# RWKV core and attention of a hybrid encoder: block-diagonal operands replaced by compact 64x64 ones, and the two pairs of heads worked in turn

## The chip, the cores and the metric

One core of one Trainium2 chip. The metric is the device time of one execution in microseconds (us), as the median of several runs; lower is better. The engines are TensorE (PE; its weight loads are PEld), VectorE (DVE), ScalarE (ACT), GpSimd (POOL) and SyncE (SP), which issues most of the transfers.

## The reference, cut to what matters

Two layers over 256 tokens of width 1024. Each layer has a token mixer and a channel mixer (a dense SwiGLU in the first layer, top-2-of-8 experts in the second), each behind a norm and a modulation from a condition vector (the "ada" weights). The token mixer projects its input (`w_in`) to four groups of 256 columns: 2-D neighbourhood attention with 4 heads of 64, bidirectional RWKV-7 with 4 heads of 64, a multi-scale pooling and a gated short convolution; the four outputs go through one output projection (`w_out`). The change touches the first two groups. RWKV is, for each head and each of the two directions:

```python
def rwkv7_step(S, inp):
    r, w, k, v, a_vec, b_vec = inp
    sa = jnp.einsum('...ij,...j->...i', S, a_vec)
    S = S * w[..., None, :] + sa[..., :, None] * b_vec[..., None, :] + v[..., :, None] * k[..., None, :]
    return S, jnp.einsum('...ij,...j->...i', S, r)
```

Attention takes for each query the keys of its row neighbourhood and 16 columns, adds a bias, and does a softmax. In the kernel that is a score matrix of 128 queries by 256 keys with a bias of -1e30 outside the window.

## The kernel before, in words

All activations are float32. Large weights come in chunks of 128 x 2048 (1 MB) through SP's queue into a ring `raw`, and are split into a high part (ScalarE, L220) and a rest (VectorE, L221); a product with them is three one-pass matmuls (`mm3`, L172). The "ada" chunks are multiplied and reduced on VectorE (L257). `mm` (L169) is a full float32 matmul.

`mixer(l)` (L361) is written as generators, one for each part of the work: `z` (RWKV projections), `q` and `r` (`rw_prep`, L470, for head pair 0 and 1), `0` and `1` (`rw_core`, L536, for pair 0 and 1), `a` (attention, L705), `p` (pooling), `c` (convolution), `f` (ada chunks as filler), `g`, and `o` (the output projection, L670). Each `yield` ends a step. A string `ORDER[l]` (L62) says which part does its next step, a letter a step; `step` (L885) first finishes the parts that one depends on (`needs`, L881). The string sets the priority; a scheduler at compile time then orders each engine's instructions by it and by when it holds their inputs to be ready. In `ORDER` of before, pair 0's core stands early, among the projections of attention, and pair 1's core late, among the output projection; each core has 41 steps.

A pair of heads is stacked on the 128 partitions: head 0 on 0 to 63, head 1 on 64 to 127. `rw_core` works on four chunks of 64 tokens (c) in two directions (e). To do both heads in one 128x128 matmul, `rw_prep` writes block-diagonal 128x128 copies of four operands (`bd4`, L374; `put_bd`, L385), with zeros from GpSimd and two ScalarE copies each. In `rw_core`:

- `s1`, `s3`, `s2` (L547 on, L580 on): products of the operands. `s1` and `s2` have 128 moving columns (two 64-column operands of `ar`).
- five levels that build the inverse of a triangular matrix (L560 on): VectorE transposes X (L563), `p1` = nT x X (L566), ScalarE copies it to P1 (L568), `p2` = XT x P1 (L573), VectorE writes it under a mask into X (L574). In the trace `p1` and `p2` are both named p.
- between the levels, transposes of three operands through TensorE (`sk`, L593).
- the recurrence over four chunks (L600 on), all in `u`: a product, a copy (L610), a product, a copy (L612), two products, and the new state (L623, L625).
- the outputs `y` (L629 on): per head a 64-column weight against 64 columns.

`slot_` (L365) gives buffers of 128 x 512 from a ring of 47. PSUM has two sets of four banks, `pa` and `pb`; pair 0's core and the RWKV projections use `pb`, attention, convolution and pooling `pa`. `bk` (L533) says which set a core takes; with `SWITCH` (0, 0) pair 1's core takes `pa` for its first step alone. The output projection holds the four banks of `pa` from its first step to the end. Attention (L705) pads the queries of each head with zeros (`qz`, L713), computes two heads' scores into one bank (L741), and multiplies with values for both heads of the pair (L759), of which half is used.

The mixers stand at the start of the two layers; the dense FFN follows the first, the experts (MoE) follow the second.

Of the kernel before, what the change touches and what calls it, by code (L numbers as in the profile page):

```python
# [48 lines left out]
_CST = [("ident", 128), ("i2", 64), ("bones", 128), ("bones64", 128), ("m1s", 256), ("m1i", 128), ("m3", 256),  # L49
# [4 lines left out]
for _n, _w in _CST:  # L54
# [22 lines left out]
def _constants():  # L77
# [10 lines left out]
    t2 = np.concatenate([t, t])  # L88
    same = h[:, None] == h[None]
    c["m1s"] = np.concatenate([same & (s[:, None] < t2), same & (s[:, None] > t2)], axis=1) * 1.0  # L90
    c["m1i"] = np.concatenate([s[:, None] <= t, s[:, None] >= t], axis=1) * 1.0
    c["m3"] = np.concatenate([same & (t2 < s[:, None]), same & (t2 > s[:, None])], axis=1) * 1.0
# [18 lines left out]
    lx = np.zeros((128, NLV + 1, 2, 128))  # L111
    for l in range(-1, NLV):
        b = 1 << (l + 1)
        sb, tb = s[:, None] // b, t2[None] // b
        up = (sb % 2 == 0) & (tb == sb + 1)
        dn = (sb % 2 == 1) & (tb == sb - 1)
        lx[:, l + 1, 0] = up & same
        lx[:, l + 1, 1] = dn & same
# [5 lines left out]
def kernel(ctx, tc, x, cc, cst, cst2, msk, ada, pcol, lora, poolw, rpb, win, winl, wout,  # L124
# [15 lines left out]
    mk = per.tile([128, (NLV + 1) * 256], U8, name="mk")  # L140
# [220 lines left out]
    def mixer(l, fillers):  # L361
        with ExitStack() as st:
# [11 lines left out]
            def bd4(name):  # L374
                b = slot_(name).rearrange("p (n h t) -> p n h t", n=4, h=2)
                pool.memset(b[0:64, :, 1, :], 0.0)
                pool.memset(b[64:128, :, 0, :], 0.0)
                return b

            def flat(b, n):  # L380
                return b[:, n].rearrange("p h t -> p (h t)")
# [3 lines left out]
            def put_bd(b, src):  # L385
                for h in range(2):
                    act.activation(b[HS[h], :, h, :], src[HS[h]], AF.Copy)
# [82 lines left out]
            def rw_prep(hp):  # L470
# [45 lines left out]
                B = {n: [] for n in "ABKV"}  # L516
# [10 lines left out]
            m1s = C("m1s").rearrange("p (e h t) -> p e h t", e=2, h=2)  # L527
            m1i = C("m1i").rearrange("p (e t) -> p e t", e=2)
            m3 = C("m3").rearrange("p (e f) -> p e f", e=2)
# [6 lines left out]
            def rw_core(hp):  # L536
                R = st_r[hp]
                ar, B, bc = R["ar"], R["B"], R["bc"]
                arb = n8("arb")
                ark = n8("ark")  # L540
                X, nT, XT, ak, sB, sK, sV, Ub, Sb = [[None, None] for _ in range(9)]
                for e in range(2):
                    X[e] = v4(slot_("X"))
                    act.activation(X[e], ident[:, None, :].to_broadcast([128, 4, 128]), AF.Copy)
                    p = bk[hp]("s1").rearrange("p (c m t) -> p c m t", c=4, m=2)
                    for c in range(4):
                        mm(p[:, c], flat(B["B"][e], c), ar[e][:, c])  # L547
# [5 lines left out]
                    for c in range(4):  # L553
                        mm(p[:, c], flat(B["A"][e], c), flat(B["B"][e], c))
# [4 lines left out]
                for lv in range(NLV):  # L559
                    pt = [None, None]  # L560
# [945 lines left out]
```

## Time and profile before

| | us |
|---|---|
| median of 3 runs | 1547.24 |
| lowest and highest | 1546.98, 1551.23 |
| the profiled execution | 1546.37 |
| its span, first to last instruction | 1544.5 |
| PE busy | 1443.1 |
| DVE busy | 645.8 |
| ACT busy | 435.5 |
| POOL busy | 24.9 |

All rows come from one profiled execution of 1546.37 us. Busy time is the union of the instructions of an engine. Matmuls are pipelined: an instruction's length reaches over the start of the next ones, so how fast a stream runs is read from the distance of their starts. A float32 matmul shows as two instructions. In a row of instructions, `128*64 128x64` after the names means 128 rows by 64 columns of weights against 64 moving columns. Tile names come without their numbers.

### The profile page before, as it was taken

Reading aid. Unit: us, or ns where it says so; the run is one execution under the profiler, and the core shown is the slowest. Engines: PE = TensorE matmul, PEld = TensorE weight load, DVE = VectorE, ACT = ScalarE, POOL = GpSimd, SP = SyncE. Lnnn points to the kernel's source line nnn. Section 1 sums busy time; section 2 is a strip of 40 time slices with the busy share of each in tenths; the row PEclk is TensorE's granted clock in tenths of the full one; section 3 lists DMA queues with packets and bytes.
Section 4 is the critical chain, followed back from the end, with each engine's and each line's share of the span. In section 5 each row is a group of like instructions: output and inputs, shape, how many; then the busy total and the mean of one; then the engine's idle time right before and its main releaser. Section 6 shows DMA issues by size and latency. Waiting matters only on the chain. (4 is left out here: it accounts for less than half of the span.)

```text
span 1544.5 us, 28342 instructions
## 1 busy us (share of the span) xinstructions
PE 1443.1 (93%) x12174; PEld 875.5 (57%) x12174; DVE 645.8 (42%) x1194; ACT 435.5 (28%) x814; POOL 24.9 (2%) x91
## 2 busy tenths in 40 slices
PE   3999989999998999989889899999999999998885
PEld 2988979999997999963223233433433234332222
DVE  7799869977856777651010021020020110110202
ACT  4854645544437746350011000010010010000101
POOL 1001000000001001000000000000000000000000
PEclk9999999999999999999999999999999999999998
DMA  9556138987743411189999999999999999999995
GB/s 373 215 204 227 55 146 340 394 339 306 293 158 122 158 55 42 45 323 363 416 415 416 417 417 417 416 415 382 412 417 416 417 415 416 416 415 416 416 410 194
DMA packets 85253, 487.79 MB, mean 316 GB/s; under 512 B 9841, under 2 KB 10225, under 8 KB 40946
## 3 DMA queue, kind: packets, MB, share of 16 engines
q1 hardware_dynamic: 83522, 482.98, 78.3%
q10 hardware_dynamic: 1584, 2.68, 0.6%
q8 instruction: 113, 1.85, 0.5%
q14 instruction: 34, 0.28, 0.0%
HBM read 484.57 MB, written 1.05 MB: 314 GB/s over the span
## 5 line engine op out<-in xcount | busy, mean ns | idle before, releaser
L170 PE MATMUL u<-mw,xe 128*32 128x512 f32 (+1 forms) x3368 | 359.0, 537 | 20.1 <-DMA mw<-in_moe_dram 18.7
L1179 DVE TENSOR_TENSOR sg<-sg,u 128x256 f32<-128x256 f32 (+1 forms) x96 | 34.3, 380 | 650.6 <-ACT sg L1178 650.6
L170 PEld LDWEIGHTS u<-mw,xe 128*32 128x32 f32 x3368 | 114.5, 109 | 220.8 <-issue 160.4
L1178 ACT ACTIVATE sg<-u 128x256 f32<-128x256 f32 (+1 forms) x96 | 30.8, 355 | 666.0 <-PE u L170 656.5
L170 PE MATMUL y<-mw,sT 128*32 128x512 f32 x1480 | 180.4, 594 | 15.5 <-DMA mw<-in_moe_dram 10.8
L221 DVE TENSOR_TENSOR wlo<-raw,whi 128x1024 fp32r<-128x1024 f32 x142 | 169.8, 1218 | 46.7 <-ACT whi L220 46.5
L220 ACT ACTIVATE whi<-raw 128x1024 fp32r<-128x1024 f32 x142 | 146.4, 1056 | 137.1 <-issue 43.6
L170 PE MATMUL u<-mwhi,xe 128*32 128x512 f32 (+1 forms) x748 | 172.6, 551 | 0.4 <-PEq L1132 0.3
L170 PE MATMUL u<-mwlo,xe 128*32 128x512 f32 (+1 forms) x748 | 150.7, 551 | 0.5 <-PEq L1132 0.2
L174 PE MATMUL g<-hlo,whi 128*128 128x256 f32 x448 | 126.9, 284 | 0.5 <-DVE hlo L339 0.3
L173 PE MATMUL g<-hhi,whi 128*128 128x256 f32 x448 | 126.9, 284 | 0.0
L175 PE MATMUL g<-hhi,wlo 128*128 128x256 f32 x448 | 126.6, 283 | 0.0
L170 PEld LDWEIGHTS y<-mw,sT 128*32 128x32 f32 x1480 | 52.5, 109 | 128.0 <-issue 84.7
L257 DVE CUSTOM_DVE_ANT_0 raw<-raw,row,pcs 128x1024 f32<-128x1024 f32 x96 | 120.3, 1278 | 4.5 <-ACT row L1362 3.9
L170 PE MATMUL y<-mwhi,sT 128*32 128x512 f32 x324 | 96.2, 594 | 0.1
L173 PE MATMUL z<-hhi,whi 128*128 128x256 f32 x304 | 88.9, 293 | 4.1 <-ACT whi L220 4.0
L170 PEld LDWEIGHTS u<-mwhi,xe 128*32 128x32 f32 x748 | 46.2, 109 | 79.7 <-issue 70.0
L175 PE MATMUL z<-hhi,wlo 128*128 128x256 f32 x304 | 88.1, 290 | 2.2 <-DVE wlo L221 2.2
L174 PE MATMUL z<-hlo,whi 128*128 128x256 f32 x304 | 87.6, 289 | 0.5 <-DVE hlo L339 0.3
L174 PEld LDWEIGHTS g<-hlo,whi 128*128 128x128 f32 x448 | 85.9, 192 | 1.6 <-DVE hlo L339 1.2
L173 PEld LDWEIGHTS g<-hhi,whi 128*128 128x128 f32 x448 | 86.0, 192 | 0.6
L175 PEld LDWEIGHTS g<-hhi,wlo 128*128 128x128 f32 x448 | 85.9, 192 | 0.0
(317 smaller groups left out, 2022.8 us busy)
## 6 DMA issues: line engine op xcount, KB each, us to landing
mw<-in_moe_dram SPq DMA_DIRECT2D x232, 1024.0 KB, 15.0
mwlo<-in_moe_dram SPq DMA_DIRECT2D x104, 512.0 KB, 12.6
mwhi<-in_moe_dram SPq DMA_DIRECT2D x104, 512.0 KB, 13.8
raw<-in_ada_dram SPq DMA_DIRECT2D x44, 1024.0 KB, 6.7
raw<-in_ffn_dram SPq DMA_DIRECT2D x42, 1024.0 KB, 7.1
raw<-in_win_dram SPq DMA_DIRECT2D x20, 1024.0 KB, 4.9
raw<-in_wout_dram SPq DMA_DIRECT2D x6, 1024.0 KB, 5.0
raw<-in_ada_dram SPq DMA_DIRECT2D x8, 512.0 KB, 7.1
```

Of the source, the lines that this page charges most:

```text
L170: pe.matmul(o, a, b, start=start, stop=stop)
L173: pe.matmul(o, ah, bh, start=start, stop=False)
L174: pe.matmul(o, ah, bl, start=False, stop=False)
L175: pe.matmul(o, al, bh, start=False, stop=stop)
L220: ops[0].append(act.activation(hi, raw[:, c], AF.Copy))
L221: ops[1].append(dve.tensor_sub(lo, raw[:, c], hi.bitcast(F32)))
L257: r = dve.tensor_tensor_reduce(w, w, cB, scale=1.0, scalar=P(l, "ab", v * KB + k), op0=OP.mult, op1=OP.add, accum_out=mods[l][:, v, k:k + 1])
L1178: other_set(act.activation(sg, u[:, 0:w], AF.Silu))
L1179: dve.tensor_mul(sg, sg, u[:, w:2 * w])
```

## The change

Every product of the RWKV core becomes two 64x64 products, for the two heads, on the two diagonal quarters of the array; the operands stay compact, 64 columns wide in place of 128, in a second ring of 38 buffers of 128 x 256 (`half`). `bd4` and `put_bd` go. The transposes `sk` become products with a 64x64 identity. Masks and constants are 64 columns wide. Attention's queries are copied in one piece; the two heads' scores are 64-row products into two banks, with two bias additions; the value product takes a head's 64 columns. `ORDER` is new: the projections first, then steps of both cores in turn. The last piece but one of the output projection is a part of its own, `O`, that waits for core 0; `o` no longer waits for it. `SWITCH` (99, 99) keeps pair 1's core on `pa` until `o` starts. The ring of 128 x 512 buffers has 36. The reserve of SBUF for descriptors is cut to 1024 bytes.

```diff
-NSLOT = 47
+NSLOT = 36
+NHALF = 38
-ORDER = (('00zzzzqqqaqaq0a00a0a0a00000pp00a000a00000pa00f000a00af00000a0000rcarf00rfrffccrcfffffo11gf'
-          '11101111111111111111111111111111111o1o1111foffoooooooofffffffffffffffff'),
-         ('zzzqqaqqfa0aqa0000pa000a0000000a00p000ap0000az00000a0a0000001crar0ra00110crr1c0go1c1111111'
-          '1111111111111111111111o11o11o11o1ooooooo'))
-SWITCH = (0, 0)
+ORDER = (('zzzzqaqaqaqrcrcrcrp00010a101a01f010f10p101a01a010f10c101a01f010f101a01p010a10f101f01a010a10f101f01a01fg'
+          '010f101o01o010f101o01o010f101o01o'),
+         ('zzzzqaqaqaqrcrcrcrp0001010a1010a1010p10101a0101a0101c01010a1010a1010p10101a0101a0101a0101a010o101o01'
+          '0o101o010o101o010o101o'))
+SWITCH = (99, 99)
...
+            def half(name):
+                return mp.tile([128, 256], F32, name=name, tag="h", bufs=NHALF).rearrange("p (n f) -> p n f", n=4)
+            def mmh(o, a, b, start=True, stop=True):
+
+                for h in HS:
+                    mm(o[h], a[h], b[h], start, stop)
...
-                for e in range(2):
-                    for n, src in (("B", c4(bc)[:, e]), ("A", ar[e][:, :, 0, :]), ("K", c4(kf)[:, e]),
-                                   ("V", c4(zv)[:, e])):
-                        b = bd4("bd" + n)
-                        put_bd(b, src)
-                        B[n].append(b)
-                    yield
-                st_r[hp] = dict(eP=eP, ar=ar, bc=c4(bc), B=B)
+                st_r[hp] = dict(eP=eP, ar=ar, B=c4(bc), K=c4(kf), V=c4(zv))
+                yield
...
-                        pt[e] = v4(bk[hp]("p1"))
+                        p = pq("p1")
                         for c in range(4):
-                            mm(pt[e][:, c], nT[e][:, c], X[e][:, c])
-                        P1[e] = v4(slot_("P1"))
-                        act.activation(P1[e], pt[e], AF.Copy)
+                            mmh(p[:, c], nT[e][:, c], X[e][:, c])
+                        P1[e] = half("P1")
+                        act.activation(P1[e], p, AF.Copy)
...
-                                pe.transpose(p[:, c], flat(B[nm][e], c), ident)
-                            b = v4(slot_("s" + nm))
+                                mmh(p[:, c], R[nm][:, e, c], C("i2"))
+                            b = half("s" + nm)
...
-                        mm(pu[:, 0], ak[e][:, c], sV[e][:, c], True, i == 0)
+                        mmh(pu[:, 0], ak[e][:, c], sV[e][:, c], True, i == 0)
...
-                    for h in range(2):
-                        for j, (a, b) in enumerate(seq):
-                            mm(yp[HS[h], c * 64:(c + 1) * 64], a[:, HS[h]], b, j == 0, j == len(seq) - 1)
+                    for j, (a, b) in enumerate(seq):
+                        mmh(yp[:, c * 64:(c + 1) * 64], a, b, j == 0, j == len(seq) - 1)
...
-                        p = pa("sc").rearrange("p (h t) -> p h t", h=2)
+                        s = et("sc")
+                        ps = [pa("sc") for _ in range(2)]
                         for h in range(2):
-                            mm(p[:, h, :], qz[hp][:, h, qs], kt[:, hp, :])
-                        s = et("sc")
-                        dve.tensor_add(s, p, bi)
+                            mm(ps[h][:, 0:T], qt[HS[h], hp, qs], kt[HS[h], hp, :])
+                        for h in range(2):
+                            dve.tensor_add(s[:, h, :], ps[h][:, 0:T], bi[:, h, :])
...
-                                mm(po[:, i, :], pt[:, h, k, :], vn[:, k, hp * 128:(hp + 1) * 128], k == 0, k == 1)
+                                mm(po[:, i, HS[h]], pt[:, h, k, :], vn[:, k, hp * 128 + 64 * h:hp * 128 + 64 * h + 64],
+                                   k == 0, k == 1)
...
-                yield from out_proj(3, yrw, False, False, 0)
...
-                     "f": fill(99), "g": gate_row(), "r": rw_prep(1), "1": rw_core(1), "o": outs()}
-            needs = {"q": "z", "0": "q", "1": "r", "r": "z", "o": "apc0", "g": "f" if l == 0 else ""}
+                     "f": fill(99), "g": gate_row(), "r": rw_prep(1), "1": rw_core(1), "o": outs(),
+                     "O": out_proj(3, yrw, False, False, 0)}
+            needs = {"q": "z", "0": "q", "1": "r", "r": "z", "o": "apc", "O": "0", "g": "f" if l == 0 else ""}
...
-    nc = _bacc.Bacc("TRN2", target_bir_lowering=False, num_devices=1)
+    nc = _bacc.Bacc("TRN2", target_bir_lowering=False, num_devices=1, dynamic_dma_scratch_size=1024)
```

## Rows read from the trace of the kernel before

**Rows 1.** Busy time by stage: a stretch in us from the span's start and its length; then for PE, PEld, DVE, ACT and POOL the busy us and the number of instructions; the granted clock, the DMA share, GB/s. The first mixer, the second, the MoE layer from 700 us on.
```profile
30.00:228.00 198.00, 186.83 (x1500) 174.30 (x1500) 161.69 (x301) 113.91 (x216) 5.03 (x18) 1.00 0.49 176
485.00:671.00 186.00, 182.44 (x1494) 171.46 (x1493) 132.87 (x241) 109.30 (x210) 5.86 (x19) 1.00 0.28 96
700.00:1544.50 844.50, 792.52 (x7247) 276.58 (x7238) 113.77 (x265) 64.18 (x163) 0.00 (x0) 1.00 0.99 404
```
**Rows 2.** What TensorE waited for in the second mixer (485 to 671 us): the waiting engine and tile, the releaser; us in total, times, longest.
```profile
PE lw L170 <- issue: 1.0, 1, 1.0
```
**Rows 3.** The timeline of PE: start, us, engine, line, operation, tiles, shape, count of the instructions merged in the row.
```profile
155.11 0.28 PE L173 MATMUL z<-hhi,whi 128*128 128x256 f32 x1
155.23 0.28 PE L174 MATMUL z<-hlo,whi 128*128 128x256 f32 x1
...
189.09 1.04 PE L593 MATMUL sk<-cs,bdK 128*128 128x128 f32 x8
189.97 1.95 PE L170 MATMUL p<-X,nT 128*128 128x128 f32 x16
191.75 1.45 PE L170 MATMUL p<-P,XT 128*128 128x128 f32 x11
...
571.83 1.03 PE L170 MATMUL sc<-kt,qz 128*128 128x256 f32 x4
572.69 1.05 PE L170 MATMUL u<-sV,ak 128*128 128x128 f32 x8
```
**Rows 4.** The timeline of PE in the output product of pair 1 in the first mixer, where it goes from head 0 to head 1 of a chunk; and one row of the view of the tile y in the first mixer, with the least, median and greatest length in ns, the first and the last start.
```profile
207.93 0.28 PE L170 MATMUL y<-ark,sV 128*64 128x64 f32 x2
...
208.16 0.22 PE L170 MATMUL y<-ark,sV 128*64 128x64 f32 x1
208.16 0.22 PE L170 MATMUL y<-ar,Sb 128*64 128x64 f32 x1
208.22 0.22 PE L170 MATMUL y<-arb,Ub 128*64 128x64 f32 x1
208.22 0.22 PE L170 MATMUL y<-ar,Sb 128*64 128x64 f32 x1
...
L170 PE MATMUL y<-arb,Ub x64: 222/222/270, 143.0 to 210.9; 128*64 128x64 f32 x64
```
**Rows 5.** The timeline of PE: two matmuls of 512 columns on the whole array in the out-projection, and the 64-row products that combine the experts' outputs in the MoE layer (`back`, L1214), which write two banks in turn; each with the row that follows it.
```profile
202.31 0.63 PE L175 MATMUL ya<-whi,ylo 128*128 128x512 f32 x2
202.77 0.38 PE L170 MATMUL u<-Sb,bdA 128*128 128x128 f32 x2
...
804.31 1.66 PE L170 MATMUL cb<-yhl,oT 64*128 64x512 f32 x11
805.90 0.64 PE L170 MATMUL u<-mw,xe 128*32 128x512 f32 x4
```
**Rows 6.** The first mixer (30 to 228 us), busy time of the instructions of one tile alone, in this order: p, s, u, sk, y, the scores sc and the out-projection ya. The columns are those of rows 1, without the engines that have none (PE, PEld, then DVE, ACT; for s PE, PEld, DVE; for sk PE, PEld, ACT). Of the 32 PE instructions of sc 16 are the scores and 16 read them for a transpose.
```profile
30.00:228.00 198.00, 39.71 (x320) 38.14 (x320) 14.30 (x20) 11.84 (x20) 1.00 0.49 176
30.00:228.00 198.00, 11.93 (x96) 11.21 (x96) 10.39 (x20) 1.00 0.49 176
30.00:228.00 198.00, 20.59 (x136) 17.79 (x136) 11.84 (x44) 0.00 (x0) 1.00 0.49 176
30.00:228.00 198.00, 6.22 (x48) 5.44 (x48) 6.52 (x12) 1.00 0.49 176
30.00:228.00 198.00, 9.20 (x176) 8.24 (x176) 0.00 (x0) 0.75 (x2) 1.00 0.49 176
30.00:228.00 198.00, 7.15 (x32) 4.56 (x32) 5.40 (x8) 4.38 (x16) 1.00 0.49 176
30.00:228.00 198.00, 26.31 (x96) 17.39 (x96) 3.56 (x6) 2.75 (x8) 1.00 0.49 176
```
**Rows 7.** The timeline of PE where the recurrence (128 columns of weights) and the output product (64) take turns.
```profile
205.35 0.39 PE L170 MATMUL u<-sV,ak 128*128 128x128 f32 x2
205.67 0.33 PE L170 MATMUL y<-ark,sV 128*64 128x64 f32 x2
205.93 0.49 PE L170 MATMUL u<-Sb,bdA 128*128 128x128 f32 x2
206.25 0.39 PE L170 MATMUL u<-tU,X 128*128 128x128 f32 x2
```
**Rows 8.** The timeline of PE in the recurrence of pair 1, first mixer: the first and the last row between which rows of ya stand ten times between rows of u.
```profile
193.60 0.83 PE L170 MATMUL u<-sV,ak 128*128 128x128 f32 x6
...
205.03 0.48 PE L170 MATMUL u<-Sb,bdA 128*128 128x128 f32 x2
```
**Rows 9.** Groups of instructions in the first mixer (30 to 228 us): line, engine, operation, tiles, out<-in shapes, count | busy us, mean ns | idle us before, and what ended it.
```profile
L574 DVE COPY_PREDICATED X<-mk,p 128x512 f32<-128x512 uint8 x20 | 14.3, 725 | 5.3 <-PE p L170 5.3
L551 DVE TENSOR_TENSOR arb<-s,cs 128x256 f32<-128x256 f32 x4 | 1.6, 412 | 0.0
L257 DVE CUSTOM_DVE_ANT_0 raw<-raw,row,pcs 128x1024 f32<-128x1024 f32 x25 | 31.5, 1272 | 0.0
L221 DVE TENSOR_TENSOR wlo<-raw,whi 128x1024 fp32r<-128x1024 f32 x31 | 37.3, 1216 | 5.3 <-ACT whi L220 5.1
L387 ACT ACTIVATE bdV<-zdv 64x256 f32<-64x256 f32 x8 | 3.3, 416 | 0.1
```
**Rows 10.** SP's issues of MoE weights behind the second mixer: start, us from the first to the end of the last of the row, count.
```profile
675.92 22.25 SPq L1006 DMA_DIRECT2D mw<-in_moe_dram  x3
```

More of the change, by code (lines that the diff above doesn't have):

```diff
@@ L87, in _constants @@
     c["bones64"] = bo / 64.0
-    t2 = np.concatenate([t, t])
-    same = h[:, None] == h[None]
-    c["m1s"] = np.concatenate([same & (s[:, None] < t2), same & (s[:, None] > t2)], axis=1) * 1.0
+    c["m1s"] = np.concatenate([s[:, None] < t, s[:, None] > t], axis=1) * 1.0
     c["m1i"] = np.concatenate([s[:, None] <= t, s[:, None] >= t], axis=1) * 1.0
-    c["m3"] = np.concatenate([same & (t2 < s[:, None]), same & (t2 > s[:, None])], axis=1) * 1.0
+    c["m3"] = np.concatenate([t < s[:, None], t > s[:, None]], axis=1) * 1.0
     tt = np.arange(T)
@@ L110, in _constants @@
     cs2 = np.concatenate([c["rst"], c["pinv"]], axis=1).astype(np.float32)
-    lx = np.zeros((128, NLV + 1, 2, 128))
+    lx = np.zeros((128, NLV + 1, 2, 64))
     for l in range(-1, NLV):
         b = 1 << (l + 1)
[L114 to L118, printed above, removed]
+        sb, tb = s[:, None] // b, t[None] // b
+        lx[:, l + 1, 0] = (sb % 2 == 0) & (tb == sb + 1)
+        lx[:, l + 1, 1] = (sb % 2 == 1) & (tb == sb - 1)
     msk = lx.reshape(128, -1).astype(np.float32)
@@ L139 @@
     cs = per.tile([128, NCST], F32, name="cs")
-    mk = per.tile([128, (NLV + 1) * 256], U8, name="mk")
+    mk = per.tile([128, (NLV + 1) * 128], U8, name="mk")
     xr = per.tile([128, 2, D], F32, name="xr")
@@ L515, in rw_prep @@
                 zv = zmix(4 + hp, "zdv")
-                B = {n: [] for n in "ABKV"}
-                for e in range(2):
-                    for n, src in (("B", c4(bc)[:, e]), ("A", ar[e][:, :, 0, :]), ("K", c4(kf)[:, e]),
-                                   ("V", c4(zv)[:, e])):
-                        b = bd4("bd" + n)
-                        put_bd(b, src)
-                        B[n].append(b)
-                    yield
-                st_r[hp] = dict(eP=eP, ar=ar, bc=c4(bc), B=B)
+                st_r[hp] = dict(eP=eP, ar=ar, B=c4(bc), K=c4(kf), V=c4(zv))
+                yield
             mx = mk.rearrange("p (l e f) -> p l e f", l=NLV + 1, e=2)
-            m1s = C("m1s").rearrange("p (e h t) -> p e h t", e=2, h=2)
+            m1s = C("m1s").rearrange("p (e t) -> p e t", e=2)
             m1i = C("m1i").rearrange("p (e t) -> p e t", e=2)
-            m3 = C("m3").rearrange("p (e f) -> p e f", e=2)
+            m3 = C("m3").rearrange("p (e t) -> p e t", e=2)
             def b4(ap):
@@ L580, in rw_core @@
                             for c in range(4):
-                                mm(p[:, c], flat(B["K"][e], c), ar[e][:, c])
+                                mmh(p[:, c], R["K"][:, e, c], ar[e][:, c])
                             dve.tensor_mul(ark[:, 4 * e:4 * e + 4, :], p[:, :, 1, :], b4(m1i[:, e, None, :]))
-                            ak[e] = v4(slot_("ak"))
-                            dve.tensor_mul(ak[e].rearrange("p n (h t) -> p n h t", h=2),
-                                           p[:, :, 0:1, :].to_broadcast([128, 4, 2, 64]),
-                                           b4(m1s[:, e, None]))
+                            ak[e] = half("ak")
+                            dve.tensor_mul(ak[e], p[:, :, 0, :], b4(m1s[:, e, None]))
                             yield
@@ L598, in rw_core @@
                 for e in range(2):
-                    Ub[e] = v4(slot_("Ub"))
-                    Sb[e] = v4(slot_("Sb"))
-                prev = [None, None]
+                    Ub[e] = half("Ub")
+                    Sb[e] = half("Sb")
                 for i in range(4):
@@ L706, in attention @@
                 p = z_pair(3, pa)
-                qz = []
-                for hp in range(2):
-                    q_ = et("qz")
-                    qz.append(q_)
-                    for h in range(2):
-                        pool.memset(q_[HS[1 - h], h, :], 0.0)
-                        act.activation(q_[HS[h], h, :], p[HS[h], hp, :], AF.Copy, scale=0.125)
+                qt = et("qt")
+                act.activation(qt, p, AF.Copy, scale=0.125)
                 yield
@@ L897, in step @@
                 seen[k] += 1
-                if k == "1" and seen[k] > SWITCH[l] or k == "o":
+                if k == "1" and seen[k] > SWITCH[l] or k in "oO":
                     bk[1] = pb
@@ L901, in step @@
                     parts[k] = None
-            for k in ORDER[l] + "zq0apcfgr1o":
+            for k in ORDER[l] + "zq0apcfgro1O":
                 step(k)
-            for k in "zq0apcfgr1o":
+            for k in "zq0apcfgro1O":
                 while parts[k] is not None:
```

60 lines of the change are left out of this document (25 added, 35 removed).

## The prediction, made before the changed kernel was run

> **What bounds the kernel now.** I read the table by stage first, to see which engine is full where. The kernel has two mixers with a dense FFN between them, and a mixture-of-experts (MoE) layer last. The last 844.5 us run at a DMA share of 0.99 and 404 GB/s: this layer is bound by its weights, so a change ahead of it moves only its start. The change touches the two mixers alone, 30 to 228 us and 485 to 671 us. In the second TensorE is busy 182.4 of 186 us, in the first 186.8 of 198; VectorE has 132.9 and 161.7 us, ScalarE some 110, DMA is at 0.28 and 0.49 [rows 1]. Then the waits of TensorE in the second mixer: the longest is 1.0 us [rows 2]. So TensorE's stream is the bound in both mixers, and what counts is the spacing of its instructions, not the length that a row gives a single one.
>
> **The spacing.** It comes from the timeline, as the time from a merged row's start to the next row's, by its count. Sixteen 128x128 matmuls take 189.97 to 191.75: 0.111 us each; eight transposes 0.88: 0.110; four with 256 columns 0.86: 0.215 [rows 3]. A float32 product is two such instructions (the levels' loops issue 160 products per mixer, p has 320 rows [rows 6]); a transpose is one. With 64 weight columns and 64 moving columns two take 0.28, at 0.222 for one: 0.058 apart [rows 4].
>
> **Do two small ones run side by side?** The core after the change issues each product as two 64x64 ones, for partitions 0 to 63 and 64 to 127, with different rows and different columns of the array. No row of before has that shape, but each half of it is there. Different columns: where the output product goes from one head to the other, pairs of starts coincide (208.16 with 208.16, 208.22 with 208.22) and the next pair follows 0.06 later, both in the same PSUM bank [rows 4]. Different rows: eleven 64-row matmuls of 512 columns take 1.59 us from their start to the next row's; two whole-array ones of 512 columns take 0.46, 0.23 each, by which eleven would need 2.5. They run in pairs, in two banks [rows 5]. I take 0.058 us for a pair of 64x64x64 passes. Bounds: 0.058 (full overlap) and 0.116 (none).
>
> **TensorE's terms, per mixer** (counts from [rows 6], the same in both):
> - p (both products of the levels), 320 x (0.111 − 0.058) = 17.0 us.
> - s, 96 in three kinds of 32: s3 shrinks, 32 x 0.053 = 1.7; the two against `ar` keep 128 moving columns, so two quarters side by side take the 0.111 of before: 0.
> - u (recurrence), 136 x 0.053 = 7.2.
> - sk: 48 transposes at 0.110 become 48 products of two passes, 96 x 0.058 = 5.6 against 5.3: −0.3.
> - y: 176 instructions, of which the weight loads cover 8.2 us; all in pairs, 88 x 0.058 = 5.1: 3.1.
> - sc: 16 of 0.215 become row pairs, 8 x 0.215: 1.7.
> - pv: 16 products (32 instructions) with 64 moving columns instead of 128, but 128 weight columns still. Between 0 and 32 x 0.053 = 1.7; the nearest rows, all with 128 weight columns, never come closer than 0.11, so 0.
>
> The sum is 30.4 us per mixer. That is the end with full overlap. With none, p would take 640 x 0.058 = 37.1 in place of 35.5, +1.6, and in the same way s3 +0.1, u +0.7, y +2.0; sk 192 x 0.058 = 11.1, +5.8; the two kinds of s against `ar` 128 x 0.111 in place of 64, +7.1: 17.3 us lost, less sc's 1.7 makes 15.6. I take the first end, as both halves of the shape are at it.
>
> **What it adds on TensorE.** The array changes shape. Around the output product, the way from the recurrence to it and back shows the price: from 205.35 to 206.25 there are two u, two y, two u, which by spacing need 4 x 0.111 + 2 x 0.058 = 0.56, and take 0.90 [rows 7]. So one excursion into another shape costs 0.34 us. Before, only y makes them. After, each run of core work between 128-wide work is one. How many? In one pair's recurrence the out-projection breaks into the u's ten times between 193.60 and 205.03 [rows 8]. The attention left over (4 score blocks, 4 sets of transposes, 4 value products) and pooling break in some 14 times; the recurrence of two pairs at once, as for one, 10 to 20. I take 36: 12.2 us per mixer. Ends: 15 (5 us), if the scheduled order keeps the core together, and 110 (37 us), if each of the 82 steps and most of the 44 recurrence groups stand alone.
>
> **The other engines.** VectorE: the 20 masked writes of the levels (0.725), their 20 transposes and 12 other operations on 512 columns, taken alike, shrink to 256, for which a row has 0.41: 52 x 0.3 = 15.6 us; the 44 copies of the recurrence (11.8 us) lose a little; the score addition is split, 4 x (2 x 0.41 − 0.72) = +0.4 [rows 9]. ScalarE loses 32 block copies of 0.416 and nearly half of 20 P and 12 transposed copies: some 20 us. GpSimd's memsets go; it is nearly idle. All of this is cover off the path, worth nothing by itself; it keeps VectorE at 117 of a second mixer that shrinks to some 172.
>
> **The order.** All ten and a half projection chunks now stand ahead of both cores; before, the first core ran beside them. Their 456 instructions and the value projection's 48, at the 0.12 from one's start to the next [rows 3], are 60 us of TensorE work, which hides the preparation of both pairs. Behind them TensorE has both cores (18.6 + 9.0 + 5.6 + 7.9 + 5.1 = 46 us after the change), the scores and value products (some 7), the out-projection (96 x 0.23 = 22 [rows 6]) and the 12 us of excursions: 88. VectorE has there, in the first mixer, 25 ada halves of 1.27 (31.5), the cores (52 + 8 operations at 0.41, some 12 us of recurrence: 37) and the splits of four output weights (8 x 1.22) [rows 6, 9]: 78 without attention. Two full engines that wait for each other lose time. I estimate 6 us there and 4 in the second mixer, where no ada work is left; bounds −5 (today's 11 us without TensorE work in the first mixer shrink) and +15. A new wait comes with the banks of PSUM: the second core keeps attention's four banks until the out-projection starts (before, it left them after its first step), and a score block takes two of them instead of one until VectorE has added the bias (2 x 0.41); queued behind such a wait on TensorE are the second core's next groups, and that is in the estimate. ScalarE's queue issues the four bias loads with the attention steps, 256 KB each, as before. SP issues the same weight loads in another order, projections before ada chunks; DMA at 0.28 to 0.49 has room. Masks and constants shrink by half a megabyte: hidden, 0. The smaller reserve of SBUF for descriptors is unused by the queues shown: 0. The last out-projection part still waits for a core, as before.
>
> **The end.** Of three MoE weights whose issue begins at 675.9 us, just behind the second mixer, the last waits for a buffer till 698, when the layer runs [rows 10]. All of this hangs on the end of the second mixer, so what the mixers save reaches the end in full.
>
> **Sum.** 2 x (30.4 − 12.2) − 10 = 26 us off. The profiled execution took 1546.4 us (span 1544.5), 0.06% under the median of the runs, 1547.2. 1546.4 − 26 = 1520, and 1521 from the median: I say **1520**. A measurement of this kernel tells 0.3% (4.6 us) from no change.
>
> **Rivals.**
> - *Shape changes decide* (slower). Price 0.34 us each; 30.4 / 0.34 = 89 per mixer is where the gain is gone. For it: the recurrence is broken into ten times by one out-projection [rows 8], and a group of one product now lasts 0.12 us. Against: the two pairs stand next to each other step by step and can fill each other's gaps. With 110 per mixer and the 10 us of the order: 2 x (37.4 − 30.4) + 10 = +24, so 1570; with 100, 1564. Chance 0.10.
> - *The halves don't run side by side*, because both write one PSUM bank from different rows: the 64-row pairs in the trace write two banks [rows 5]. Nor does [rows 4] show more than three pairs in a row. Then 2 x (15.6 + 12.2) + 10 = +66, 1612. Against: column halves share a bank in pairs [rows 4], and row halves keep it up for eleven. Chance 0.05. The Trainium skill, "TensorEngine Tiling (Array Packing)", section "Restrictions and Gotchas", states that different row tiles cannot access the same PSUM bank at the same time; by that rule this rival is the outcome, and no run here shows the case of different rows and different columns.
> - *The order gives it back*: VectorE bounds the second part of the first mixer and the recurrences come last with little beside them; each mixer loses a further 10 us: 1540. With 15: 1550. For it: VectorE's 161.7 of 198 [rows 1]. Against: it sheds 15 us too. Chance 0.14, most of it within 0.3%.
> - *More comes through*: 15 excursions per mixer and no loss by order: 2 x (30.4 − 5) = 51, 1495. For it: the scheduler already gets 182 of 186 us. Chance 0.12.
>
> **Numbers.** The forecast, 1500 to 1540, has 0.59. Faster by over 0.3%: 0.59 + 0.12 + 0.05 of the order case = 0.76; same 0.09; slower 0.15. The range leaves out the two slow cases' far parts and a little at the fast end: 1488 to 1553.
>
> **What would show it.** In the changed profile: pairs of 64*64 rows starting together and the next pair 0.058 later, else the second rival; 0.2 us and 0.15 us steps at each change to 128-wide rows, and their number, for the first; both mixers 10 to 19 us shorter with TensorE still over 0.9 busy; if its share falls below that while VectorE's rises, the order decides. PEclk at 1.00 through both mixers; a fall there would be a cost that I have not counted. The MoE stage must keep 844 us to within a few; if not, the end does not follow the mixers.

## The result, and the profile after

The changed kernel takes **1510.31 us** (median of 4 runs, 1509.55 to 1513.13), the kernel before in the same session 1547.11 us (1546.45 to 1551.23): ratio 0.976, 95% interval 0.9739 to 0.9781. It is 37 us faster; the forecast was 1520 with a range of 1488 to 1553.

The profiled execution took 1509.55 us, its span is 1507.8. Lined up from the first projection (z) to the last output projection (ya), the first mixer went from 196.4 us to 175.9 (−20.5), the second from 185.0 to 168.1 (−16.9). What lies ahead is 0.6 us shorter, the FFN between the mixers 0.3 us, and the part behind the second mixer is 1.6 us longer (874.0 to 875.6). That adds up to −36.7, the whole difference of the spans.

Busy time by stage in the changed kernel, columns as in [rows 1]: the first mixer, the second, all that follows.

```profile
30.00:207.00 177.00, 168.14 (x2196) 147.48 (x2196) 143.66 (x304) 90.88 (x180) 0.00 (x0) 0.99 0.54 193
464.00:633.00 169.00, 165.57 (x2197) 144.22 (x2196) 113.52 (x242) 87.59 (x174) 0.52 (x1) 1.00 0.32 114
632.20:1507.80 875.60, 810.80 (x7395) 294.19 (x7419) 131.46 (x330) 79.50 (x201) 0.00 (x0) 0.99 0.98 398
```

Against [rows 1], TensorE is busy 18.7 us less in the first mixer (186.8 to 168.1) and 16.9 in the second (182.4 to 165.6); the forecast had 18.2 for each. Between the first z and the last ya it stands idle for 7.8 us of the first mixer (9.6 before) and 3.4 of the second (3.4). The last row is the part bound by weights, which kept its length.

The instructions of p and of u alone, in the first mixer; columns PE, PEld, DVE and ACT, then as above.

```profile
30.00:207.00 177.00, 26.79 (x640) 23.73 (x640) 8.70 (x20) 7.64 (x20) 0.99 0.54 193
30.00:207.00 177.00, 13.27 (x272) 10.33 (x272) 8.81 (x44) 0.00 (x0) 0.99 0.54 193
```

Twice the instructions of [rows 6] take two thirds of the busy time (39.7 and 20.6 us there), and the 20 masked writes of VectorE went from 14.3 us to 8.7. How dense the stream is shows in the timeline of TensorE in the second mixer: start, us, then engine, line, operation, tiles, shape and the count of merged instructions.

```profile
545.93 0.73 PE L167 MATMUL p<-P,XT 64*64 64x64 f32 x17
546.45 0.27 PE L167 MATMUL s<-ar,kf 64*64 64x128 f32 x1
...
546.96 0.22 PE L167 MATMUL p<-X,nT 64*64 64x64 f32 x1
546.96 0.22 PE L167 MATMUL p<-P,XT 64*64 64x64 f32 x1
```

Seventeen starts in 0.52 us are 0.031 us each, so 0.061 for two quarters side by side; [rows 3] had 0.111 for the pass that they replace. The two last rows are a pair that starts within 2 ns.

The price of a change of shape, where the output projection breaks into the recurrence of the second mixer (same view):

```profile
602.10 0.40 PE L171 MATMUL ya<-wlo,yhi 128*128 128x512 f32 x1
602.43 0.33 PE L167 MATMUL u<-sV,sK 64*64 64x64 f32 x4
602.59 0.28 PE L167 MATMUL u<-Ub,sB 64*64 64x64 f32 x4
602.81 0.50 PE L172 MATMUL ya<-whi,ylo 128*128 128x512 f32 x1
603.14 0.39 PE L170 MATMUL ya<-whi,yhi 128*128 128x512 f32 x1
603.37 0.39 PE L171 MATMUL ya<-wlo,yhi 128*128 128x512 f32 x1
```

A ya pass has 0.23 us from start to start (603.14 to 603.37). The last before the u's takes 0.33, the first after them 0.33 again; eight u's, 0.23 at the ordinary spacing, take 0.38. One excursion costs 0.10 + 0.15 + 0.10 = 0.35 us here. There are 37 excursions into 64x64 in the first mixer and 39 in the second.

One cost was not in the forecast: part of the first mixer ran at the lower clock. Two stretches of the first mixer, columns as above:

```profile
126.00:134.00 8.00, 6.30 (x190) 5.79 (x184) 7.91 (x21) 3.84 (x10) 0.00 (x0) 1.00 0.36 141
134.00:142.00 8.00, 7.99 (x103) 5.67 (x99) 6.47 (x15) 3.07 (x9) 0.00 (x0) 0.79 0.36 137
```

TensorE was busy 6.3 of 8 us, and then the granted clock is 0.79 on the mean of the next 8: 3.4 us at 1.2 GHz instead of 2.4, about 1.7 us of work. The stretch from 158 to 166 us was busy 6.4 of 8 us, and the clock stayed at 1.00 in it and behind it, so these rows do not show what brings it down. Before, the clock was 1.00 through both mixers [rows 1].

### The profile page after: what moved, and what is told of

It is laid out like the page before. It is cut to its first block, busy times and chain, and to the rows that moved or that the text cites. A ratio compares the mean times of both kernels' runs of the same rounds, so it can differ in the third digit from the quotient of the medians.

```text
span 1507.8 us, 30915 instructions
## 1 busy us (share of the span) xinstructions
PE 1400.7 (93%) x13541; PEld 824.0 (55%) x13566; DVE 609.9 (40%) x1202; ACT 391.9 (26%) x744; POOL 1.8 (0%) x19
## 5 line engine op out<-in xcount | busy, mean ns | idle before, releaser
L167 PE MATMUL y<-mw,sT 128*32 128x512 f32 x1480 | 180.9, 594 | 18.7 <-DMA mw<-in_moe_dram 13.4
## 6 DMA issues: line engine op xcount, KB each, us to landing
mwlo<-in_moe_dram SPq DMA_DIRECT2D x104, 512.0 KB, 12.6
```

Source lines behind the costliest of these rows:

```text
L167: pe.matmul(o, a, b, start=start, stop=stop)
```

## The experiments

All are edits of the changed kernel. Times are medians beside the 1510.31 us of the changed kernel; the ratio is to the kernel before, measured on the same chip in the same session. The kernel before had medians of 1546.9 to 1548.3 us in these sessions, so a difference of a microsecond or two from the changed kernel is not shown by the medians alone. Where lengths of mixers and busy times are given without a fence, they run from the first z to the last ya of the profiled execution.

### Do the two quarters work side by side?

`headwise` and `pairs2` change only which product follows which, in all groups but the recurrence:

```diff
-                for c in range(4):
-                    mmh(p[:, c], nT[e][:, c], X[e][:, c])
+                mmg([(p[:, c], nT[e][:, c], X[e][:, c], True, True) for c in range(4)])
...
+            def mmg(ops):                       # headwise
+                for h in HS:
+                    for o, a, b, start, stop in ops:
+                        mm(o[h], a[h], b[h], start, stop)
...
+                for i in range(0, len(ops), 2):  # pairs2
+                    for h in HS:
+                        for o, a, b, start, stop in ops[i:i + 2]:
+                            mm(o[h], a[h], b[h], start, stop)
```

> All groups of the core that hold several products (levels, operand products, transposes by products, outputs) issue head 0's products first and then head 1's, so that neighbours in the stream use the same quarter of the array; the recurrence, the order of the steps and the number of instructions stay. Theory (the gain comes from two quarters working side by side): a 64-column pass then takes 0.058 us by itself instead of 0.031; 640 + 64 + 192 + 176 such passes lose 0.027 each (29 us) and 128 passes of 128 columns lose 0.055 (7 us), less one boundary in eight that still overlaps: 32 us per mixer, some 1574 us in all, and at least 1550. Rival (the quarter is fast by itself, whichever neighbour it has): 0.031 stays, 1505 to 1515 us.

Measured: 1529.05 us, ratio 0.988 (0.9859 to 0.9901); TensorE is busy 11.2 and 11.0 us longer in the two mixers. The theory holds in direction, its size does not: 18.7 us instead of 64, and less than the 40 that it had named as the least. TensorE in `headwise`, second mixer:

```profile
552.00 0.27 PE L167 MATMUL p<-P,XT 64*64 64x64 f32 x1
552.05 0.22 PE L167 MATMUL p<-X,nT 64*64 64x64 f32 x1
552.11 0.22 PE L167 MATMUL p<-P,XT 64*64 64x64 f32 x1
552.11 0.22 PE L167 MATMUL p<-X,nT 64*64 64x64 f32 x1
552.17 0.22 PE L167 MATMUL p<-P,XT 64*64 64x64 f32 x1
552.17 0.22 PE L167 MATMUL p<-X,nT 64*64 64x64 f32 x1
552.22 0.56 PE L167 MATMUL p<-P,XT 64*64 64x64 f32 x10
552.58 0.27 PE L167 MATMUL p<-X,nT 64*64 64x64 f32 x1
```

Sixteen starts in 0.58 us: two blocks of eight in the time of ten passes of 0.058. At each seam some three instructions of the next quarter start beside the last of the old one (552.11 with 552.11, 552.17 with 552.17); the others stand alone. So instructions overtake the other quarter by a few places, and only a long block of one quarter loses the overlap. `pairs2` tests that reading:

> As the run headwise, but the heads alternate every two products (four instructions of one quarter, then four of the other) instead of every four (eight and eight). In headwise, in a stretch of p alone, eight starts of a quarter took 0.29 us instead of 0.46, so three of eight instructions had found the other quarter's stream. Theory (a quarter's stream runs ahead of the other by some three instructions, whatever stands between): blocks of four are then nearly covered, at most one of four alone: 0.031 to 0.036 us per instruction, 1508 to 1516 us. Rival (a share of each block overlaps, so the block's length does not matter): 0.042 as in headwise, 1529 us.

Measured: 1510.89 us, ratio 0.9765 (0.9747 to 0.9784): no loss. TensorE in the same place:

```profile
552.24 0.63 PE L167 MATMUL sk<-cs,zdv 64*64 64x64 f32 x15
552.65 0.57 PE L167 MATMUL p<-P,XT 64*64 64x64 f32 x13
```

Fifteen starts in 0.41 us, 0.027 each: blocks of four are covered in full. So at least half of the 37 us (18.7) is the overlap of the quarters, and it needs the two heads near each other in the stream, not strictly in turn.

### What does a change of shape cost?

Whole-array products that nobody reads, put into the middle of the level groups; `dum40x1` one in every group, `dum10x4` four in every fourth, `dumsmall` one of 64x64 in every group:

```diff
                         for c in range(4):
                             mmh(p[:, c], nT[e][:, c], X[e][:, c])
+                            if c == 1:
+                                dummy()   # mm(bank[:, 256:320], ident, C("i2"))
+                                          # dumsmall: mm(bank[0:64, 256:320], i2[0:64], i2[0:64])
```

> Adds work: in the middle of each of the 40 level groups of a mixer stands one more whole-array product (identity times 64 columns, two instructions, written into unused columns of the same bank, read by nobody): 80 products. The scheduled order has 76 and 75 excursions into 64x64 where the changed kernel has 37 and 39: 75 more. Theory (a change of shape costs 0.34 to 0.44 us): own work 160 x 0.12 = 19 us, excursions 75 x 0.34 to 0.44 = 26 to 33 us, so +45 to +52: 1555 to 1562 us. Rival (changes of shape cost next to nothing on the path, the gain was limited by something else): +19 at most, 1529 us or less.

> Adds the same 80 whole-array products as the run with one at each of 80 places, but four at a time at every fourth place: 50 and 47 excursions by the scheduled order, 21 more than in the changed kernel. Theory: own work 19 us and 21 x 0.34 to 0.44 = 7 to 9 us: +26 to +28, 1536 to 1538 us; so 54 excursions fewer than its sister should save 18 to 24 us. Rival (only the work counts): the same time as its sister.

> Adds 80 products at the same 80 places, but of 64x64 on one quarter of the array (identity times 64 columns): work without a change of shape; 37 and 35 excursions. Theory: 160 instructions at 0.031 to 0.058 us = 5 to 9 us, less 4 excursions (1.5 us): +3 to +8, 1513 to 1518 us. Rival (any instruction put into the middle of a group costs what the whole-array one does): +26 us or more.

Measured: `dum40x1` 1538.41 (0.9938, 0.9916 to 0.9959), `dum10x4` 1524.38 (0.9853, 0.9831 to 0.9874), `dumsmall` 1510.66 (0.9757, 0.9735 to 0.9778). The traces have 76 and 75, 50 and 47, 37 and 35 excursions. TensorE in `dum10x4` and then in `dum40x1`, second mixer:

```profile
547.34 0.40 PE L167 MATMUL p<-P,XT 64*64 64x64 f32 x8
547.67 1.10 PE L167 MATMUL p<-cs 128*128 128x64 f32 x8
548.70 0.45 PE L167 MATMUL p<-P,XT 64*64 64x64 f32 x8
548.98 0.63 PE L167 MATMUL p<-X,nT 64*64 64x64 f32 x16
```

```profile
553.42 0.40 PE L167 MATMUL p<-P,XT 64*64 64x64 f32 x8
553.75 0.43 PE L167 MATMUL p<-cs 128*128 128x64 f32 x2
554.11 0.45 PE L167 MATMUL p<-P,XT 64*64 64x64 f32 x8
```

Eight added instructions take 1.03 us to the next start and two take 0.36: 0.112 each and 0.14 for the change. Ahead of them the eight p take 0.33, not 0.23: another 0.10; and the eight p behind them take 0.28 (548.70 to 548.98), 0.05 more. That is 0.29 us per excursion. The two runs with the same 80 products, `dum10x4` and `dum40x1`, differ by 54 excursions alone and by 15.6 us of busy TensorE, 0.29 us each, and by 14.0 us of time, 0.26 each. So a change of shape costs a little less than the forecast's 0.34 beside short passes, and that much beside those of 512 columns.

All three came out below what was expected, for two reasons. The price of 0.34 to 0.44 was too high: by the rows `dum40x1` adds 80 x 0.223 + 75 x 0.29 = 39.6 us instead of 45 to 52, and TensorE is busy 35.9 us more; what the other 3.7 are stays open. And idle time was filled: 5.0 us of its two mixers are without TensorE work, 11.2 in the changed kernel, so the mixers grew by 29.7 only. In `dumsmall` TensorE is busy 4.3 us longer; the median grew by 0.4 and the span of the profiled execution by 2.4. So this kernel takes up some 2 to 6 us of added TensorE work in its idle time.

### Operands or order?

`oldorder` has the compact operands in the order of before:

```diff
-ORDER = (('zzzzqaqaqaqrcrcrcrp00010a101a01f010f10p101a01a010f10c101a01f010f101a01p010a10f101f01a010a10f101f01a01fg'
...
+ORDER = (('00zzzzqqqaqaq0a00a0a0a00000pp00a000a00000pa00f000a00af00000a0000rcarf00rfrffccrcfffffo11gf'
...
-SWITCH = (99, 99)
+SWITCH = (0, 0)
...
+                yield from out_proj(3, yrw, False, False, 0)     # inside outs() again, "o" needs "apc0"
```

> Compact operands in the order of before: ORDER, SWITCH (0, 0), the last part but one of the output projection inside o again, which waits for core 0. Everything else as in the changed kernel. The scheduled order has 38 and 49 excursions into 64x64, 11 more than the changed kernel. Theory (the operands bring the gain, the order next to nothing): 11 x 0.26 to 0.31 = 3 us more, and no more idle TensorE than before had (11 and 4 us): 1511 to 1518 us. Rival 1 (the turn by turn order brings a good part, as one pair alone cannot keep TensorE busy any more): 1525 us or more. Rival 2 (the new order costs, as my forecast had it with 10 us): 1500 to 1505 us.

Measured: 1521.69 us, ratio 0.9837 (0.9814 to 0.986): the order, with the banks and the place of `O` that go with it, is worth 11 us of the 37, between the theory and rival 1, and the opposite of rival 2. The first mixer is 9.9 us longer than in the changed kernel, the second 2.6. Busy time in three stretches of its first mixer, and the timeline of TensorE in the first two of them (in brackets the idle time before a row and its releaser):

```profile
86.00:94.00 8.00, 4.00 (x46) 3.14 (x42) 6.14 (x12) 2.24 (x7) 0.00 (x0) 0.72 0.51 185
94.00:102.00 8.00, 8.00 (x67) 7.01 (x67) 5.69 (x16) 1.09 (x4) 0.00 (x0) 0.64 0.58 209
158.00:166.00 8.00, 5.18 (x31) 3.65 (x28) 7.44 (x17) 2.49 (x4) 0.00 (x0) 0.79 0.57 218
```

```profile
85.81 1.10 PE L167 MATMUL p<-X,nT 64*64 64x64 f32 x32
90.22 1.18 PE L731 MATMUL pT<-cs,sc 128*128 128x128 f32 x4 [3.31 <-ACT sc L725]
92.09 1.97 PE L167 MATMUL pv<-vn,pt 128*128 128x64 f32 x8 [0.69 <-ACT pt L733]
93.99 1.23 PE L167 MATMUL sc<-kt,qt 64*128 64x256 f32 x4
```

With one pair of heads at a time the smaller products are done before VectorE and ScalarE have the next operands ready. TensorE waits 3.3 us for one softmax and 2.8 us in the second place, and is idle for 12.6 us of the mixer (7.8 with the new order). Near the end of such a wait the clock falls: means of 0.72 and 0.64 in two stretches, and the eight pv that take 1.04 us to the next start elsewhere take 1.90 here (92.09 to 93.99, the start of the next row). The three stretches lack 0.28, 0.36 and 0.21 of 8 us, the clock of some 7 us of work, part of it idle anyway; the changed kernel lacks 1.7.

`switch0` changes the banks alone: `SWITCH = (0, 0)`, the second core on the first core's four banks.

> The changed kernel with SWITCH (0, 0): the second core takes the first core's four banks of PSUM from its second step on, not those of attention. Scheduled order with 34 and 40 excursions (37 and 39 before). Theory (banks are part of my estimate of the order's loss, and hold up little): within 4 us, 1507 to 1515 us. Rival (two cores on the same four banks wait for each other, so separate banks are a good part of what the order brings): 1518 us or more.

Measured: 1514.17 us, ratio 0.9784 (0.9762 to 0.9806), +3.9: at the edge of the theory and below the rival. In the profiled execution the first mixer is 3.5 us longer (179.4 us against 175.9), the second 0.2. Its first mixer, columns as in [rows 1]:

```profile
30.00:210.00 180.00, 169.48 (x2196) 149.29 (x2196) 142.97 (x302) 90.54 (x180) 0.00 (x0) 0.95 0.52 188
```

TensorE is idle 9.8 us there (7.8 in the changed kernel), and the mean of the clock is 0.95 instead of 0.99: 17 us of the mixer ran at 1.2 GHz, 3.4 in the changed kernel. So banks of its own for the second core are not most of the order's gain; whether they are any part of it is not shown, as the lower clock alone, part of which fell into waits, could make up the 3.5 us.

`lessdve` leaves out part of the computation, the ada reductions of the first mixer on three quarters of their columns:

```diff
-            r = dve.tensor_tensor_reduce(w, w, cB, scale=1.0, scalar=P(l, "ab", v * KB + k),
...
+            nw = D // 4 if hold.get("mix") else D
+            r = dve.tensor_tensor_reduce(w[:, 0:nw], w[:, 0:nw], cB[:, 0:nw], scale=1.0, scalar=P(l, "ab", v * KB + k),
...
```

> The changed kernel with a part of the computation left out: the reductions of the ada weights that fill the first mixer work on 256 of 1024 columns, so VectorE has some 24 us less work there (25 of 1.27 us to about a quarter); transfers, TensorE's work and the order stay. Theory (TensorE's stream is the bound of the first mixer): 0 to -4 us, 1506 to 1511 us. Rival (VectorE is a second bound in the first mixer, which keeps TensorE idle for 8 of its 176 us): -5 to -8 us, 1502 to 1505 us.

Measured: 1634.75 us, but that total says nothing, as other modulation values lead to other work in the MoE layer. Busy time in the two mixers, and the page's row on all transfers, here and (second fence) in the changed kernel:

```profile
30.00:207.00 177.00, 169.28 (x2196) 148.73 (x2196) 126.05 (x303) 89.99 (x181) 0.00 (x0) 0.98 0.52 192
DMA packets 93049, 531.64 MB, mean 326 GB/s; under 512 B 10705, under 2 KB 11089, under 8 KB 44882
```

```profile
DMA packets 85262, 487.43 MB, mean 323 GB/s; under 512 B 9841, under 2 KB 10225, under 8 KB 40946
```

44 MB more are fetched, and the part behind the second mixer takes 1000 us instead of 876. The first mixer can be compared: VectorE lost 17.6 us of work in it (first z to last ya), and it took 176.0 us against 175.9. VectorE is no second bound. TensorE had the lower clock for 6.8 us of it, 3.4 in the changed kernel, which hides 1.7 us at most, less than the rival's 5.

`olast` takes the output projection out of the recurrences:

```diff
-'010f101o01o010f101o01o010f101o01o'
+'010f10101010f10101010f10101'        # the tail of ORDER[0]; the same in ORDER[1]
```

> The changed kernel with all steps of the output projection taken out of ORDER, so that they follow behind the last core step; nothing else. 25 and 22 excursions by the scheduled order, 29 fewer. Theory (with the price of 0.31 us measured for a break by 512 columns): 9 us saved, and the recurrences, whose four chains have no other work beside them, leave TensorE idle for 3 to 8 us per mixer: between -3 and +8 us, 1507 to 1518. Rival 1 (changes of shape decide): 1501 to 1504 us. Rival 2 (cover decides, the chains of copies last far longer than TensorE's work): 1525 us or more.

Measured: 1506.19 us, ratio 0.9732 (0.9713 to 0.9751), −4.1: below the theory's range, above rival 1. Busy time in its two mixers:

```profile
30.00:209.00 179.00, 166.28 (x2196) 148.36 (x2196) 143.16 (x303) 91.21 (x183) 0.00 (x0) 0.99 0.53 189
467.00:630.00 163.00, 159.53 (x2196) 144.23 (x2196) 114.39 (x245) 88.06 (x176) 0.53 (x1) 0.99 0.28 101
```

In the second mixer 17 excursions went and 5.9 us with them: 0.35 each, the price read above, and not a microsecond of new idle time. The four chains of two pairs keep TensorE busy by themselves, so the output projection between them was no cover but a cost. In the first mixer 12 excursions went and TensorE is busy 1.9 us less, 0.16 for each, which stays open; its idle time rose from 7.8 to 11.0 us, and the mixer is 1.4 us longer.

### Attention, and versions that go further

`attold` has the attention of before (padded queries, one score bank, values for both heads):

```diff
-                            mm(ps[h][:, 0:T], qt[HS[h], hp, qs], kt[HS[h], hp, :])
+                            mm(p[:, h, :], qz[hp][:, h, qs], kt[:, hp, :])
```

> The changed kernel with the attention of before: queries padded with zeros, both heads' scores in one bank, value products for both heads. Core and order stay as changed. Theory (the forecast's terms): the score pairs are worth 8 x 0.215 = 1.7 us per mixer and the value products nothing: +3.4 us, 1513 to 1515 us. Rival 1 (the attention's part is hidden in idle TensorE): within 1.5 us of the changed kernel. Rival 2 (one score bank instead of two frees the second core's banks earlier): 1506 to 1508 us.

Measured: 1511.94 us, ratio 0.976 (0.9741 to 0.978), within what can be told from no change. A score block of four in `attold` and (second fence) in the changed kernel, in the second mixer:

```profile
540.20 1.13 PE L167 MATMUL sc<-kt,qz 128*128 128x256 f32 x4
541.26 0.45 PE L167 MATMUL p<-X,nT 64*64 64x64 f32 x8
```

```profile
539.89 0.70 PE L167 MATMUL sc<-kt,qt 64*128 64x256 f32 x4
540.53 0.27 PE L167 MATMUL p<-X,nT 64*64 64x64 f32 x2
```

The block takes 1.06 us to the next start and 0.63 in the changed kernel, so the pairs save the 1.7 us per mixer that the forecast gave them. The second mixer is 1.7 us longer in `attold`; the first ends at 206.0 us of the span instead of 205.9 (its first z starts 2.0 us later, at 32.0). The saving is there on TensorE; that it reaches the end is not shown.

`pvcol` cuts each value product into two column halves:

```diff
-                                mm(po[:, i, HS[h]], pt[:, h, k, :], vn[:, k, hp * 128 + 64 * h:hp * 128 + 64 * h + 64],
-                                   k == 0, k == 1)
+                                for q in HS:
+                                    mm(po[q, i, HS[h]], pt[:, h, k, q],
+                                       vn[:, k, hp * 128 + 64 * h:hp * 128 + 64 * h + 64], k == 0, k == 1)
```

> The changed kernel with each value product of attention (128x128 weights, 64 moving columns) cut into two of 64 weight columns, on the two column halves of the array, which start together where y did so in the kernel before. Theory: 32 instructions per mixer of 0.112 us become 32 pairs of 0.058: 1.7 us per mixer, -3.4 us, 1506 to 1508 us, and TensorE's starts show the pairs. Rival 1 (the gain falls into idle TensorE): within 1.5 us. Rival 2 (the shape 128*64 between 64*64 and 128*128 costs more changes, up to one per product group, 8 x 0.2 us per mixer): +1 to +3 us.

Measured: 1505.97 us, ratio 0.9727 (0.9707 to 0.9748), −4.3 us, as the theory said; in the profiled execution the mixers are 1.7 and 1.6 us shorter. A block of value products in the changed kernel and (second fence) in `pvcol`:

```profile
544.89 1.10 PE L167 MATMUL pv<-vn,pt 128*128 128x64 f32 x8
545.93 0.45 PE L167 MATMUL p<-P,XT 64*64 64x64 f32 x8
```

```profile
543.56 0.69 PE L167 MATMUL pv<-vn,pt 128*64 128x64 f32 x16
544.17 0.44 PE L167 MATMUL p<-P,XT 64*64 64x64 f32 x7
```

1.04 us become 0.61, for eight blocks 3.4 us. `better` adds to it:

```diff
-                mm(p[:, 0:T], C("bones64"), y)
+                for h in HS:
+                    mm(p[h, 0:T], C("bones64")[h, h], y[h])
...
-                mm(p[:, T:2 * T], lr[:, 4, hp * 128:(hp + 1) * 128], lin[:, 0, :])
+                pg = bk[hp]("bg")
+                for h in range(2):
+                    mm(pg[HS[h], 0:T], lr[HS[1], 4, hp * 128 + 64 * h:hp * 128 + 64 * h + 64], lin[HS[1], 0, :])
...
-                    mm(p[:, b, :], pw[:, b, :], d[:, b, :])
+                    for h in HS:
+                        mm(p[h, b, :], pw[h, b, h], d[h, b, :])
```

> The kernel of pvcol with three more products cut into 64x64 ones, all with weights that are zero outside the two head blocks: the sums over a head (gm, bo), the gate of RWKV (its own bank, two column quarters of the lower rows) and the pooling weights (pp). A 256-column pass of two halves side by side lasts as long as one of the whole array, so only changes of shape go: 33 and 37 excursions into 64x64 by the scheduled order, counted as the changed kernel's 37 and 39, so 6 fewer. Theory: 6 x 0.26 to 0.31 = 1.7 us less than pvcol, some 1504 us, and -5 us against the changed kernel. Rival (the changes that go were covered by waits, these products stand at the ends of chains): the time of pvcol within 1 us.

Measured: 1505.80 us, ratio 0.973 (0.9712 to 0.9748), the time of `pvcol`, as the rival had it. The six excursions went, but the trace also shows two of the gate's four passes of 256 columns starting 0.215 us apart with nothing beside them, some 0.4 us for each core. The clock is lower too: its mean is 0.97 in the first mixer and 0.98 in the second, 0.99 in both for `pvcol`. So why the six excursions gave nothing is not shown. Three versions came out 4 to 4.5 us below the changed kernel, `pvcol`, `better` and `olast`. That is at the edge of what the medians can tell (their intervals overlap with the changed kernel's, 0.9739 to 0.9781); for `pvcol` and for the second mixer of `olast` the traces bear it out. `pvcol` and `olast` touch different terms, but together they were not tried.

## Why the prediction was right, and where it was not

**The bound.** Right: TensorE's stream decides. VectorE with 18 us less work in the first mixer changed nothing there (`lessdve`), while a seam in the stream (`headwise`) and added passes (`dum40x1`) moved the time.

**Side by side.** Right: 0.061 us a pair where 0.058 was taken. At 0.061 p saves 320 x 0.050 = 16 us of the 17.0 forecast; its busy time, which also holds waits inside the groups and changes of shape, fell by 12.9 us in the first mixer and 13.7 in the second. The rival of the PSUM bank fell: the pairs write one bank, start within 2 to 7 ns and run at full speed. The Trainium skill, "TensorEngine Tiling (Array Packing)", section "Restrictions and Gotchas", has it that different row tiles cannot access one bank at the same time; for quarters that differ in rows and in columns the trace shows otherwise.

**Smaller terms.** The scores were right on TensorE (0.43 us a block), the value products too (0.112 us each, no gain); that column halves would give the latter a gain was to be had from [rows 4] and I did not see it.

**Changes of shape.** Right in price (0.29 to 0.35 for 0.34) and in number (37 and 39 for 36), so 11 to 14 us a mixer were given back. The net of both, 18.2 us of busy time forecast for each mixer, came as 18.7 and 16.9.

**The order.** This term was wrong, in sign: I charged 6 and 4 us, and TensorE's idle time fell by 1.8 us in the first mixer and stayed in the second. That is the distance from 1520 to 1510, and it also took the first mixer past the 10 to 19 us that I had named as a sign (20.5). I had reasoned from two full engines that wait for each other, and compared the new order with TensorE's idle time of before. `oldorder` is the right comparison: with small products the order of before would have cost 12.6 us of idle time and a lower clock in the first mixer. By `oldorder` the two parts of the change belong together: with one pair in flight the smaller products gave 11 us less. What the new order does to the operands of before was not tried.

**The end.** Right to 1.6 us: what the mixers saved arrived. **The clock** was the cost that I named and did not count: some 1.7 us in the first mixer.

## What to carry to other kernels

Block-diagonal operands on TensorE can be replaced by one product per block on its own part of the array: two quarters ran in the time of one (0.058 to 0.061 us for a pair), if the blocks stand within a few instructions of each other in the stream. Count the changes of array shape (about 0.3 us each here), and do not let a filler of another shape break into a stream that keeps TensorE busy by itself. When products shrink, ask again whether the chain behind them still has enough work in flight: the order that was there for the large products, with its banks, cost 11 us with the small ones.

## What the runs showed of the hardware that I had not expected

- A quarter's instructions overtake the other's: blocks of four per quarter run at 0.027 us per instruction, as if strictly in turn; of blocks of eight, three overlap and the rest stand alone (0.036 in the rows above).
- The cost of a change of shape lies in three places: 0.10 us ahead of the first whole-array pass, 0.14 within the run of whole-array passes and behind it (0.20 where they have 512 columns), and 0.05 in the first pair of quarters. It is the same for a run of two instructions and of eight (0.36 = 2 x 0.112 + 0.14, 1.03 = 8 x 0.112 + 0.14).
- The granted clock fell to 1.2 GHz inside the mixers, where the kernel before had none of that: in `oldorder` near the end of a wait of 3.3 us, in the changed kernel in the 8 us that follow a stretch with TensorE busy 6.3 of 8. What brings it down is not shown: in the kernel before it stayed at 1.00 behind a wait of 2.3 us (108.8 to 111.1). In `oldorder` a block of value products took 1.90 us to the next start there instead of 1.04.
